# Half of the recurrent merge gate by seven products instead of eight, woven into the branch projections, with one pool for weights and activations

## The chip, the cores and the metric

The kernel runs on one core of a Trainium2 chip. Times are device microseconds of one launch. Its engines are TensorE (PE, matrix products), VectorE (DVE), ScalarE (ACT), GpSimd (POOL) and SyncE (SP, here only a queue that issues transfers). Each runs its own instructions in the order in which they were written, and waits on semaphores for the others.

## The reference

One encoder block on 256 tokens of width 2048, in fp32. `u`, `g_lru` and so on are column blocks of one input projection of width 13312.

```python
xn = rms_norm(x, norm_pre_w);  z = xn @ w_in
u_lru, g_lru, q, k, v, g_attn, m_lru, m_attn = jnp.split(z, split_at, axis=-1)
u = centred_depthwise_conv(u_lru, conv_w, conv_b)                # 4 taps
h = rg_lru(u, ..., reverse=False) + rg_lru(u, ..., reverse=True) # gates, then a scan over tokens
y_a = h * silu(g_lru)
q, k = partial_rope(q), partial_rope(k)                          # 16 heads, 4 kv heads of 128
y_b = windowed_gqa(q, k, v, sink) * silu(g_attn)                 # |i-j| <= 128
merged = sigmoid(m_lru) * (y_a @ w_proj_a) + sigmoid(m_attn) * (y_b @ w_proj_b)
out = x + rms_norm(merged @ w_out, norm_post_w)
```

## The kernel before

All products are fp32 by three: weights and activations are split into a high part (a cast to fp32r) and a low part (the rest), and a product is wh·xh + wh·xl + wl·xh.

*Steps and halves.* The weights come from DRAM in steps of 1 MB, in the order of a plan (`load_plan`). Each step has two halves of 128 x 1024. For each half ACT casts `wh` from the raw weights (line L229, issued four halves ahead) and DVE subtracts `wl` (L231, three halves ahead), and then PE multiplies. There are three kinds of step:

- `blk`: one block of 128 output columns, weights stationary. A step has 16 matmuls of 512 columns (high and low activations side by side, L261) and 16 of 256 columns (low weights, L259).
- `quad`: a quarter of the rows for 512 output columns, activations stationary, 24 matmuls of 512 columns (L234 to L236). Four quads make a chunk.
- `part`: half of one of the seven products of a `Seven`, 12 matmuls of 512 columns.

A `Seven` computes a 256 x 2048 by 2048 x 1024 product, cut into 2 x 2 blocks, by seven block products m1 to m7 instead of eight. Its activations are four blocks of x or sums of them (s1 to s4, made by `sums_of`), its weights are blocks or sums of blocks. The sums of weights are made on the way in: a cell (`x` or `y`) holds two 512 KB tiles, and transfers issued on POOL add the next block to it in place. Two Sevens exist: `am`, the second half of the attention merge gate, and `om`, the first half of w_out.

*Ticks.* Everything that isn't a step's own work is a function filed under a tick, `at(tick, fn)`, and is written out when the half of that number is written. In each half come, in this order: transfers for the step three ahead (and accumulates for the step five ahead), the functions due, the cast of the half four ahead, the subtract of the half three ahead, and the half's matmuls. That order is the order on every engine; nothing is moved later.

*Stages.* First the first four pairs' inputs `u` (quads); then for i = 0 to 7 pairs of `blk` steps for the two gates gl and ga and for u, with the recurrent pairs (`lru_pair(n, b)`: conv at b, gates' products, sigmoids, decays, `scans` at b+18, output) spread over ticks; then k, v; then q with the 16 heads, between them chunks of the recurrent gate (ml) and of w_proj_a (pa); then the attention gate (ma and the Seven `am`) with w_proj_b (pb); then w_out. A head filed at b has its scores on PE at b, exponentials on ACT at b+2, `normalise` at b+3 (DVE divides the probabilities p by their sum, L820), `flip` at b+5 (PE transposes p into pt), and `values` at b+9. A conv is four taps on DVE: L626 multiplies and adds the bias, L628 adds the other three. `x_sums(q)` makes the sums of x for the Seven: an addition of high and low part (L337), three more operations (L319 to L321) and, a tick later, the split into parts; it stores them to DRAM (`away`), and `x_sums_back` loads them when they are needed.

*Memory.* Activations live in a ring of 34 units of 4 KB a partition, raw weights in three tiles of 8 KB, `wh` and `wl` in five tiles each of 4 KB. In PSUM there are four single banks and two pairs of banks.

Of the kernel before, what the change touches and what calls it, by code (L numbers as in the profile page):

```python
# [27 lines left out]
UNITS = 34  # L29
# [4 lines left out]
LRU0 = 12  # L34
# [41 lines left out]
def load_plan():  # L76

    plan = []

    def quad(m, c):  # L80
        plan.extend(("quad", m, c, i) for i in range(4))

    def pair(m, c, n):
        plan.extend(("blk", m, c + (n + i) * P, 0) for i in range(2))

    def mixed(m, c, order):
        for o in order:
            a, i = o.split(".")
            if a in SEVEN:
                plan.append(("part", m, c, a, int(i)))  # L90
            else:
                w, w0 = CHUNKS[a[0]]
                plan.append(("quad", w, w0 + int(a[1]) * 512, int(i)))

    quad("w_in", U0)
    for i in range(8):
        if i in EARLY:
            quad("w_in", ML0 + EARLY.index(i) * 512)
        pair("w_in", GL0, 2 * i)
# [6 lines left out]
    for i in range(4):
        pair("w_in", Q0, 4 * i)
        pair("w_in", Q0, 4 * i + 2)
        quad(*MID[i])
    for m, c in MID[4:]:  # L110
        quad(m, c)
    mixed("w_in", MA0 + 1024, GATE)
    mixed("w_out", 0, OUT)
# [15 lines left out]
def body(ctx, tc, x, xT, wall, wlru, pvec, npost, ident_d, mask_d, rope_d, out):  # L129
# [3 lines left out]
    ring = ctx.enter_context(tc.tile_pool(name="ring", bufs=3))  # L133
# [55 lines left out]
    flat = lambda t: t.rearrange("p a b -> p (a b)")  # L189
# [12 lines left out]
    def cell(i):  # L202
        m, c, a, q = plan[i][1:]
        return groups[m, c].cells[SEVEN[a][1], q]

    def chained(i):
        return plan[i][0] == "part" and SEVEN[plan[i][3]][1] != "z"

    def fetch(i, lead):
        if i >= len(plan) or i in raws:  # L210
            return
        if chained(i):
            if lead == 5 and plan[i][3] in ("m6", "m7", "m4"):
                load(cell(i), plan[i], True)
        elif lead == 3:
            raws[i] = ring.tile([P, 2048], F32, tag="raw", name=f"raw{i}", bufs=3)
            nc.sync.dma_start(raws[i], wall[row[content(plan[i])]])

    def split(q, c=0, w=1024, cast=nc.scalar.copy, only=None):
# [6 lines left out]
        raw = flat(cell(i)[h]) if chained(i) else raws[i][:, h * 1024:(h + 1) * 1024]  # L226
        hs, ls, raw = wh[:, c:c + w], wl[:, c:c + w], raw[:, c:c + w]
# [5 lines left out]
    def mm3(ps, wh, wl, xh, xl, start, stop):  # L233
        nc.tensor.matmul(ps, wh, xh, start=start, stop=False)  # L234
        nc.tensor.matmul(ps, wh, xl, start=False, stop=False)  # L235
        nc.tensor.matmul(ps, wl, xh, start=False, stop=stop)  # L236
# [73 lines left out]
    def sums_of(name, src, sums, psum):  # L310
# [3 lines left out]
        f = half_unit(f"{name}f", "uu", F32).rearrange("p a (b c) -> p (a b) c", b=2)  # L314
        t = unit(name, F32R, (P, 4, 2, P))
        sums[int(name[2:])] = t

        def make(a21):
# [3 lines left out]
            soon(lambda: parts_of(t[:, :, 0], t[:, :, 1], f))  # L322

# [8 lines left out]
    away = [dram.tile([P, 4 * 2 * P], F32, name=f"away{q}") for q in range(8)]  # L332
    xsum = {}

    def x_sums(q):
        a = half_unit(f"xa{q}", "uu", F32)
        nc.vector.tensor_tensor(a, xs[q][:, :, 0].bitcast(F32), xs[q][:, :, 1].bitcast(F32), ALU.add)  # L337
        sums_of(f"xx{q}", a, xsum, False)
        soon(lambda: nc.sync.dma_start(away[q], xsum.pop(q).rearrange("p a b c -> p (a b c)").bitcast(F32)), 3)

    def x_sums_back(q):
        xsum[q] = unit(f"xb{q}", F32R, (P, 4, 2, P))
        nc.sync.dma_start(xsum[q].rearrange("p a b c -> p (a b c)").bitcast(F32), away[q])

    class Seven:
# [3 lines left out]
        def __init__(self, name, m, c, act, sums, done, double=True):  # L349
            self.name, self.act, self.sums, self.done, self.double = name, act, sums, done, double  # L350
            self.weights, self.cells, self.ps = ("part", m, c), {}, {}
            groups[m, c] = self
# [3 lines left out]

        def start(self, where, q):

            self.cells[where, q] = [unit(f"{self.name}{where}{q}{h}") for h in "ab"]
            load(self.cells[where, q], (*self.weights, "m1" if where == "x" else "m3", q))  # L360

        def second(self, q):

            load(self.cells["x", q], (*self.weights, "m5", q), True)

        def rows(self, a, i):
            if a[0] == "a":
                t, b = int(a[1]) - 1, int(a[2]) - 1
                src = self.act[i][:, b, :, t * P:(t + 1) * P]
            else:  # L370
                src = self.sums[i][:, SUMS.index(a)]
            return src[:, 0], src[:, 1]

        def half(self, m, q, h, wh, wl):
            fresh, last = q == 0 and h == 0, q == 1 and h == 1
            if fresh and self.double and m in ("m5", "m3"):

                if m == "m5":
                    self.pair = banks(f"{self.name}{m}", (P, 2, 512))
                self.ps[m] = self.pair[:, int(m == "m3")]  # L380
            elif fresh:
                self.ps[m] = bank(f"{self.name}{m}", (P, 512))
            for j in range(2):
                ah, al = self.rows(SEVEN[m][0], 4 * q + 2 * h + j)
                sl = slice(j * 512, (j + 1) * 512)
                mm3(self.ps[m], ah, al, wh[:, sl], wl[:, sl], fresh and j == 0, last and j == 1)
# [3 lines left out]
        def temp(self, name):  # L390
            return small.tile([P, 512], F32, tag="uu", name=f"{self.name}{name}", bufs=2)

        def after(self, m):
            ps, done = self.ps, self.done
            if m == "m1":
                self.m1 = small.tile([P, 512], F32, tag="upad", name=f"{self.name}c", bufs=2)
                nc.scalar.copy(self.m1, ps.pop("m1"))
            elif m == "m2":
                done(0, 0, ps.pop("m2"), self.m1, 1)
            elif m == "m6":  # L400

                self.u = small.tile([P, 512], F32, tag="upad", name=f"{self.name}u", bufs=2)
                nc.vector.tensor_tensor(self.u, ps.pop("m6"), self.m1, ALU.add)
                v = self.temp("v")
                nc.vector.tensor_tensor(v, ps["m5"], self.u, ALU.add)
                done(0, 1, ps.pop("m3"), v, -1)
# [28 lines left out]
    raws[0] = ring.tile([P, 2048], F32, tag="raw", name="raw0", bufs=3)  # L435
    for j in range(4):
        (nc.scalar if j == 1 else nc.sync).dma_start(xt[0][:, j], xT[0, :, j])
        nc.sync.dma_start(raws[0][:, j * 512:(j + 1) * 512], wall[0, :, j * 512:(j + 1) * 512])
    for i in (1, 2):
        for j in (0, 2):  # L440
            nc.sync.dma_start(xt[i][:, j:j + 2], xT[i, :, j:j + 2])
            if j == 0:
                raws[i] = ring.tile([P, 2048], F32, tag="raw", name=f"raw{i}", bufs=3)
            for c in ((j, j + 1), (j + 1, j + 2)) if i == 1 else ((j, j + 2),):
                cs = slice(c[0] * 512, c[1] * 512)
                nc.sync.dma_start(raws[i][:, cs], wall[i, :, cs])
# [111 lines left out]
    def scaled(dst, ps, then=lambda: None):  # L558
# [47 lines left out]
    def lru_pair(n, b):  # L606
# [12 lines left out]
        def conv(j):  # L619
# [6 lines left out]
            nc.vector.tensor_scalar(u, up[:, j, 0:S], cw[:, 0:1], cb, ALU.mult, ALU.add)  # L626
# [480 lines left out]
```

## Time and profile before

| | before |
|---|---|
| median of 3 runs | 900.45 us (899.63 to 901.24) |
| profiled execution | 899.96 us, span 898.2 us, clock 0.998 |
| PE busy | 888.4 us (99%), 4614 matmuls |
| DVE busy | 712.8 us (79%) |
| ACT busy | 572.4 us (64%) |
| POOL busy | 30.7 us (3%) |
| DMA | 197.38 MB, mean 220 GB/s |

The span runs from the first to the last instruction, and the profiled time is 1.8 us longer. Busy times of different engines overlap. A row of a group gives line, engine, operation, out<-in, count, then busy time and the mean of one in ns, then idle time before it. A row of a timeline or a chain gives the start and the length in us. A row of windows gives the stretch, its length, and for each engine the busy time with its instruction count.

### The profile page before, as it was taken

Reading aid. Unit: us, or ns where it says so; the run is one execution under the profiler, and the core shown is the slowest. Engines: PE = TensorE matmul, PEld = TensorE weight load, DVE = VectorE, ACT = ScalarE, POOL = GpSimd, SP = SyncE. Lnnn points to the kernel's source line nnn. Section 1 sums busy time; section 2 is a strip of 40 time slices with the busy share of each in tenths; the row PEclk is TensorE's granted clock in tenths of the full one; section 3 lists DMA queues with packets and bytes.
Section 4 is the critical chain, followed back from the end, with each engine's and each line's share of the span. In section 5 each row is a group of like instructions: output and inputs, shape, how many; then the busy total and the mean of one; then the engine's idle time right before and its main releaser. Section 6 shows DMA issues by size and latency. Waiting matters only on the chain.

```text
span 898.2 us, 12207 instructions
## 1 busy us (share of the span) xinstructions
PE 888.4 (99%) x4614; PEld 761.6 (85%) x4614; DVE 712.8 (79%) x1006; ACT 572.4 (64%) x798; POOL 30.7 (3%) x56
## 2 busy tenths in 40 slices
PE   9999999999999999999999999999999999999996
PEld 8888888888898898888888888888888888888885
DVE  6896978697979889887788979866667569778786
ACT  7688586858677977854655445554566556545764
POOL 0000000000000000000000000000002110001200
PEclk9999999999999999999999999999999999999999
DMA  9764555546465463555655455455899898797992
GB/s 338 256 237 176 190 208 191 189 158 213 158 229 185 179 211 141 188 193 205 217 183 207 169 170 205 171 204 175 280 388 261 294 292 255 260 318 264 225 312 94
DMA packets 35963, 197.38 MB, mean 220 GB/s; under 512 B 4000, under 2 KB 4768, under 8 KB 17856
## 3 DMA queue, kind: packets, MB, share of 16 engines
q1 hardware_dynamic: 30720, 179.06, 54.9%
q0 software_dynamic: 4608, 16.78, 9.9%
q10 hardware_dynamic: 576, 0.76, 0.3%
q8 instruction: 36, 0.59, 0.3%
q14 instruction: 23, 0.19, 0.1%
HBM read 190.29 MB, written 6.29 MB: 219 GB/s over the span
## 4 chain that ended last, share of the span: by engine, by line
PE 98%; DMA 1%; DVE 0%; ACT 0%; SPq 0%; DVEq 0%; issue 0%
PE q L261 7%; PE ga L261 7%; PE gl L261 7%; PE u L261 5%; PE gl L259 3%; PE ga L259 3%; PE q L259 3%; PE u L259 3%; PE u_ps L529 2%; PE k L261 2%; PE omm L235 1%; PE omm L236 1%; PE amm L235 1%; PE amm L236 1%; PE omm L234 1%; PE amm L234 1%
## 5 line engine op out<-in xcount | busy, mean ns | idle before, releaser
L229 ACT CAST wh<-raw 128x1024 fp32r<-128x1024 f32 (+1 forms) x291 | 300.0, 1041 | 178.9 <-PE q L261 25.6
L231 DVE TENSOR_TENSOR wl<-raw,wh 128x1024 fp32r<-128x1024 f32 (+1 forms) x292 | 348.1, 1204 | 67.8 <-ACT wh L229 65.3
L261 PE MATMUL q<-xs,wh 128*128 128x512 f32 x256 | 62.8, 391 | 0.0
L261 PE MATMUL ga<-xs,wh 128*128 128x512 f32 x256 | 62.4, 391 | 0.0
L261 PE MATMUL gl<-xs,wh 128*128 128x512 f32 x256 | 62.4, 391 | 0.0
L261 PEld LDWEIGHTS gl<-xs,wh 128*128 128x128 f32 x256 | 46.9, 188 | 9.0
L261 PEld LDWEIGHTS ga<-xs,wh 128*128 128x128 f32 x256 | 46.9, 188 | 8.9
L261 PEld LDWEIGHTS q<-xs,wh 128*128 128x128 f32 x256 | 46.7, 188 | 8.8
L261 PE MATMUL u<-xs,wh 128*128 128x512 f32 x192 | 46.8, 391 | 0.0
L261 PEld LDWEIGHTS u<-xs,wh 128*128 128x128 f32 x192 | 35.2, 188 | 6.7
L259 PE MATMUL q<-xs,wl 128*128 128x256 f32 x256 | 34.4, 284 | 0.0
L259 PEld LDWEIGHTS q<-xs,wl 128*128 128x128 f32 x256 | 33.1, 191 | 1.3
L259 PEld LDWEIGHTS gl<-xs,wl 128*128 128x128 f32 x256 | 33.0, 191 | 1.2
L259 PEld LDWEIGHTS ga<-xs,wl 128*128 128x128 f32 x256 | 33.0, 191 | 1.2
L259 PE MATMUL gl<-xs,wl 128*128 128x256 f32 x256 | 33.7, 283 | 0.0
L259 PE MATMUL ga<-xs,wl 128*128 128x256 f32 x256 | 33.5, 283 | 0.0
L259 PEld LDWEIGHTS u<-xs,wl 128*128 128x128 f32 x192 | 24.8, 191 | 0.9
L259 PE MATMUL u<-xs,wl 128*128 128x256 f32 x192 | 25.2, 283 | 0.0
L628 DVE SCALAR_TENSOR_TENSOR uu<-upad,pv,uu 128x256 f32<-128x256 f32 x48 | 23.3, 485 | 2.3
L651 ACT ACTIVATE gr<-gate,pv 128x256 f32<-128x256 f32 x32 | 15.3, 477 | 4.7 <-PE gate L236 4.7
L236 PE MATMUL gate<-ul,lwl 128*128 128x256 f32 x64 | 18.1, 283 | 0.0
L235 PE MATMUL gate<-ul,lwh 128*128 128x256 f32 x64 | 18.1, 283 | 0.0
(507 smaller groups left out, 2099.3 us busy)
## 6 DMA issues: line engine op xcount, KB each, us to landing
raw<-wall_dram SPq DMA_DIRECT2D x141, 1024.0 KB, 4.8
lraw<-wlru_dram SPq DMA_DIRECT2D x8, 512.0 KB, 5.7
away<-xx SPq DMA_DIRECT2D x8, 512.0 KB, 2.7
xb<-away SPq DMA_DIRECT2D x8, 512.0 KB, 7.1
raw<-wall_dram SPq DMA_DIRECT2D x8, 256.0 KB, 5.2
xr<-x_dram SPq DMA_DIRECT2D x4, 512.0 KB, 13.4
amx0a<-wall_dram POOLq DMA_DIRECT2D x3, 512.0 KB, 7.9
amx0b<-wall_dram POOLq DMA_DIRECT2D x3, 512.0 KB, 10.1
```

The source lines that it names most:

```text
L229: cast(hs, raw)
L231: nc.vector.tensor_tensor(ls, raw, hs.bitcast(F32), ALU.subtract)
L234: nc.tensor.matmul(ps, wh, xh, start=start, stop=False)
L235: nc.tensor.matmul(ps, wh, xl, start=False, stop=False)
L236: nc.tensor.matmul(ps, wl, xh, start=False, stop=stop)
L259: nc.tensor.matmul(ps[:, 1], wl[:, sl], a[:, 0], start=False, stop=False)
L261: nc.tensor.matmul(ps, wh[:, sl], a, start=k == 0, stop=k == KT - 1)
L529: nc.tensor.matmul(ups[b // 2][:, b % 2, m], w[:, sl], a[:, n], start=k == 0 and w is wh and m == 0, stop=stop)
L628: nc.vector.scalar_tensor_tensor(u, up[:, j, tap:tap + S], cw[:, tap:tap + 1], u, ALU.mult, ALU.add)
L651: nc.scalar.activation(v["gr"][:, 2 * d + j], ps[:, 0], AF.Sigmoid, bias=pv[:, PV_BR + b:PV_BR + b + 1])
```

## The change

- The second half of the recurrent merge gate (columns 1024 to 2047 of ml, two chunks of quads) becomes a third Seven, `L`. Its 14 parts stand between the `blk` steps of i = 2 to 7 (`EARLY_L`). The plan has 170 steps instead of 164: 64 quads (72 before), 64 blks, 42 parts (28 before). The names of the others are now `A` and `O`.
- A part's two halves share one tick. The recurrent pairs start at ticks 12, 28, 45, 62, 78, 93, 108 and 121 (before 12, 28, 44, 60, 76, 88, 100 and 112).
- The sums of x are made at ticks 24, 30, 36, 42, 48, 54, 60 and 65 instead of between the q steps. They are stored in another layout, and a part that needs sums loads its 512 KB (`x_sum`), four steps ahead: eight loads for `L` and eight for `A`. In these two m1's weights are the first content of cell `x`, and m5's are added to it.
- One pool of 50 units of 4 KB holds activations, raw weights, `wh` and `wl`. A raw step is two tiles and two 512 KB transfers. SP issues 357 transfers instead of 216, and POOL 48 accumulates instead of 32.
- The products m6, m7 and m4 accumulate in m1's bank and m3 in m5's, and ACT copies what is needed of a bank before the next is added. A Seven has three operations on DVE for its sums (seven before) and three copies on ACT (one before).
- The first tap of a conv goes from DVE to ACT, the other three come a tick later. The second half of the gates' products comes a tick later, and what follows it too.
- The row scaling of q falls away: its factor goes into the scale of the scores' reduction (`rtok_sc`). Normalising goes from DVE (b+3) to ACT (b+4); the flip on PE stays at b+5, values come at b+10.
- The order of the last stages is one list: q0 p0 q1 p1 q2 p2 q3 p3 and then the attention gate's chunks, parts and w_proj_b. So no chunk of ml stands among the q steps.

The core of the diff:

```diff
-UNITS = 34
+UNITS = 50
-MID = [("w_in", ML0 + 1024), ("w_proj_a", 0), ("w_proj_a", 512), ("w_in", ML0 + 1536), ("w_proj_a", 1024),
-       ("w_proj_a", 1536)]
+EARLY_L = {(2, 3): "m1.0", (2, 5): "m1.1", (3, 1): "m2.0", (3, 3): "m2.1", (3, 5): "m5.0", (4, 1): "m5.1", (4, 3): "m3.0",
...
+XSUM = (24, 30, 36, 42, 48, 54, 60, 65)
+LRU = (12, 28, 45, 62, 78, 93, 108, 121)
+SEVENS = {"L": ("w_in", ML0 + 1024), "A": ("w_in", MA0 + 1024), "O": ("w_out", 0)}
...
+        for j, c in enumerate([GL0 + 2 * i * P, GA0 + 2 * i * P] + [U0 + (2 * i + 4) * P] * (i < 6)):
+            for n in range(2):
+                plan.append(("blk", "w_in", c + n * P, 0))
+                if (i, 2 * j + n) in EARLY_L:
+                    a, q = EARLY_L[i, 2 * j + n].split(".")
+                    plan.append(("part", "L", a, int(q)))
...
-    ring = ctx.enter_context(tc.tile_pool(name="ring", bufs=3))
+    def raw_units(i):
+        raws[i] = [unit(f"raw{i}_{h}", F32, (P, 1024)) for h in range(2)]
+        return raws[i]
...
-            parts[q] = [ring.tile([P, 1024], F32R, tag=f"w{s}", name=f"w{s}{i}_{h}", bufs=5) for s in "hl"]
+            parts[q] = [unit(f"w{s}{i}_{h}", F32R, (P, 1024)) for s in "hl"]
...
+            b = {"m6": "m1", "m7": "m1", "m4": "m1", "m3": "m5"}.get(m, m)
+            fresh, last = q == 0 and h == 0 and b == m, q == 1 and h == 1
...
-            nc.vector.tensor_scalar(u, up[:, j, 0:S], cw[:, 0:1], cb, ALU.mult, ALU.add)
-            for tap in range(1, 4):
-                nc.vector.scalar_tensor_tensor(u, up[:, j, tap:tap + S], cw[:, tap:tap + 1], u, ALU.mult, ALU.add)
+            nc.scalar.activation(u, up[:, j, 0:S], AF.Identity, bias=cb, scale=cw[:, 0:1])
+            def taps():
+                for tap in range(1, 4):
+                    nc.vector.scalar_tensor_tensor(u, up[:, j, tap:tap + S], cw[:, tap:tap + 1], u, ALU.mult, ALU.add)
+            soon(taps)
...
+    for n in range(8):
+        behind(XSUM[n], lambda n=n: x_sums(n))
...
-            for t in range(2):
-                nc.vector.tensor_scalar(v["p"][:, t], v["p"][:, t], rd[:, t:t + 1], None, ALU.mult)
+            soon(lambda: [nc.scalar.activation(v["p"][:, t], v["p"][:, t], AF.Copy, scale=rd[:, t:t + 1]) for t in range(2)])
...
-            at(b + 9, values)
-            at(b + 10, gate_out)
+            at(b + 10, values)
+            at(b + 11, gate_out)
```

Where the order on an engine moves, first DVE behind the scans of the first recurrent pair (gr0, its last scan and the sum of both directions in sg0; `uu2` is the conv of the second pair, lwl2 and ul2 its gates' weights and inputs, wl16_1 the second half of step 16). Before:

```order
L673 SCALAR_TENSOR_TENSOR gr0_724<-a0_811,gi0_725 128x256
L231 TENSOR_TENSOR wl16_1_974<-raw16_888,wh16_1_973 128x1024
L162 TENSOR_TENSOR lwl2_1000<-lraw2_840,lwh2_999 128x1024
L231 TENSOR_TENSOR wl17_0_1003<-raw17_934,wh17_0_1002 128x1024
L678 TENSOR_TENSOR gr0_724<-gr0_724 128x512
L679 TENSOR_TENSOR sg0_730<-gr0_724,sg0_730 128x512
L162 TENSOR_TENSOR ul2_1022<-uu2_936,ul2_1022 128x512
L231 TENSOR_TENSOR wl17_1_1026<-raw17_934,wh17_1_1025 128x1024
```

The same place on DVE after the change (xa1 and xx1 are x_sums 1):

```order
L659 SCALAR_TENSOR_TENSOR uu2_971<-upad2_463,pv_73,uu2_971 128x256 x3
L232 TENSOR_TENSOR wl16_1_1006<-raw16_1_917,wh16_1_1005 128x1024
L340 TENSOR_TENSOR xa1_1043<-xs1_137 128x512
L321 TENSOR_TENSOR xa1_1043<-xa1_1043 128x256
L322 SCALAR_TENSOR_TENSOR xa1_1043<-xa1_1043 128x128
L323 SCALAR_TENSOR_TENSOR xa1_1043<-xa1_1043 128x128
L161 TENSOR_TENSOR lwl2_1034<-lraw2_859,lwh2_1033 128x1024
L232 TENSOR_TENSOR wl17_0_1040<-raw17_0_967,wh17_0_1039 128x1024
L709 TENSOR_TENSOR gr0_728<-gr0_728 128x512
L710 TENSOR_TENSOR sg0_734<-gr0_728,sg0_734 128x512
L161 TENSOR_TENSOR ul2_1065<-uu2_971,ul2_1065 128x512
L161 TENSOR_TENSOR xx1_1045<-xa1_1043,xx1_1045 128x4x128
```

The four operations of x_sums 1 now stand between two subtracts, its split follows, and the last three taps come behind the scans.

On DVE ahead of the scans of the third pair (gr4, gi4, th4), after the change; wl31 reads the cell tiles Lx1a and Lx1b, so step 31 is a woven part:

```order
L232 TENSOR_TENSOR wl31_0_1825<-Lx1a_1711,wh31_0_1824 128x1024
L698 SCALAR_TENSOR_TENSOR th4_1783<-gr4_1679,th4_1783 128x1024
L741 TENSOR_TENSOR sg4_1791<-sg4_1791,sig4_1850 128x512
L232 TENSOR_TENSOR wl31_1_1853<-Lx1b_1712,wh31_1_1852 128x1024
L232 TENSOR_TENSOR wl32_0_1879<-raw32_0_1814,wh32_0_1878 128x1024
L340 TENSOR_TENSOR xa6_1903<-xs6_264 128x512
L321 TENSOR_TENSOR xa6_1903<-xa6_1903 128x256
L322 SCALAR_TENSOR_TENSOR xa6_1903<-xa6_1903 128x128
L323 SCALAR_TENSOR_TENSOR xa6_1903<-xa6_1903 128x128
L232 TENSOR_TENSOR wl32_1_1900<-raw32_1_1815,wh32_1_1899 128x1024
L232 TENSOR_TENSOR wl33_0_1935<-raw33_0_1872,wh33_0_1934 128x1024
L726 TENSOR_TENSOR gi4_1680<-gi4_1680,th4_1783 128x1024
```

Before, these rows held the subtracts of two `blk` steps, the conv of the fourth pair and gi4, and neither a part's subtracts nor sums of x.

On ACT at the first head (p0, its exponentials and the normalising with rd0), after the change:

```order
L870 ACTIVATE p0_4699,dn0_4703<-p0_4699,nm0_4701 128x256 x2
L871 ACTIVATE es0_4702<-nm0_4701,pv_73 128x2
L597 COPY q1f0_4734<-q10_4631 128x512
L230 CAST wh90_0_4736<-raw90_0_4668 128x1024
L230 CAST wh90_1_4761<-raw90_1_4669 128x1024
L878 ACTIVATE p0_4699<-p0_4699,rd0_4757 128x256 x2
L230 CAST wh91_0_4797<-raw91_0_4727 128x1024
L230 CAST wh91_1_4832<-raw91_1_4728 128x1024
L160 CAST ph0_4856<-pt0_4817 128x2x256
```

Before, the same place on ACT had casts alone between exponentials and ph0, the cast that follows the flip:

```order
L811 ACTIVATE p0_4150,dn0_4154<-p0_4150,nm0_4152 128x256 x2
L812 ACTIVATE es0_4153<-nm0_4152,pv_82 128x2
L568 COPY q1f0_4185<-q10_4076 128x512
L229 CAST wh76_0_4187<-raw76_4114 128x1024
L229 CAST wh76_1_4216<-raw76_4114 128x1024
L229 CAST wh77_0_4248<-raw77_4179 128x1024
L229 CAST wh77_1_4283<-raw77_4179 128x1024
L161 CAST ph0_4305<-pt0_4268 128x2x256
```

The two scalings (L878) have come in behind the casts of the tick before, with one half's cast between them and the tick of the flip.

More of the change, by code (lines that the diff above doesn't have):

```diff
@@ L33 @@
 G = 1
-LRU0 = 12
 HEAD0 = 5
@@ L105, in load_plan @@
     quad("w_in", V0)
[L106 to L113, printed above, removed]
+    for o in MERGE + OUT:
+        a, i = o.split(".")
+        if a[0] in SEVENS:
+            plan.append(("part", a[0], a[1:], int(i)))
+        elif a[0] == "q":
+            plan.append(("blk", "w_in", Q0 + (4 * int(a[1]) + int(i)) * P, 0))
+        else:
+            w, c = CHUNKS[a[0]]
+            plan.append(("quad", w, c + int(a[1]) * 512, int(i)))
     return plan
@@ L169, in body, with ticks @@
     now = [0]
+    def ticks(i=None):
+        return sum(1 if p[0] == "part" else 2 for p in plan[:len(steps) if i is None else i])
     def at(hs, fn):
@@ L200, in body @@
     groups = {}
-    def cell(i):
-        m, c, a, q = plan[i][1:]
-        return groups[m, c].cells[SEVEN[a][1], q]
     def chained(i):
-        return plan[i][0] == "part" and SEVEN[plan[i][3]][1] != "z"
+        return plan[i][0] == "part" and groups[plan[i][1]].where(plan[i][2]) != "z"
     def fetch(i, lead):
-        if i >= len(plan) or i in raws:
+        if i >= len(plan):
             return
[L212 to L217, printed above, removed]
+        if plan[i][0] == "part":
+            groups[plan[i][1]].fetch(plan[i], lead)
+        if lead == 3 and i not in raws and not chained(i):
+            load(raw_units(i), plan[i])
     def split(q, c=0, w=1024, cast=nc.scalar.copy, only=None):
@@ L308, in body, with sums_of @@
     SUMS = ("s3", "s1", "s2", "s4")
-    def sums_of(name, src, sums, psum):
+    def sums_of(name, src, done, f=None):
         a = src.rearrange("p a b -> p (a b)")
@@ L329, in sums_of @@
             make(a21)
[L332 to L343, printed above, removed]
+    away = [dram.tile([P, 4, 4, 2 * P], F32, name=f"away{q}") for q in range(2)]
@@ L345, in body, with __init__ @@
     class Seven:
[L349 to L352, printed above, removed]
+        def __init__(self, name, act, sums, done):
+            self.name, self.act, self.sums, self.done = name, act, sums, done
+            self.cells, self.ps, self.kept, self.ready = {}, {}, {}, set()
+            groups[name] = self
@@ L357, in start @@
         def start(self, where, q):
             self.cells[where, q] = [unit(f"{self.name}{where}{q}{h}") for h in "ab"]
-            load(self.cells[where, q], (*self.weights, "m1" if where == "x" else "m3", q))
+            load(self.cells[where, q], ("part", self.name, "m1" if where == "x" else "m3", q))
         def second(self, q):
-            load(self.cells["x", q], (*self.weights, "m5", q), True)
-        def rows(self, a, i):
+            load(self.cells["x", q], ("part", self.name, "m5", q), True)
@@ L383, in half @@
+            if fresh:
+                self.ps[b] = bank(f"{self.name}{m}", (P, 512))
             for j in range(2):
-                ah, al = self.rows(SEVEN[m][0], 4 * q + 2 * h + j)
+                ah, al = self.rows(m, q, 2 * h + j)
                 sl = slice(j * 512, (j + 1) * 512)
-                mm3(self.ps[m], ah, al, wh[:, sl], wl[:, sl], fresh and j == 0, last and j == 1)
+                mm3(self.ps[b], ah, al, wh[:, sl], wl[:, sl], fresh and j == 0, last and j == 1, b != m)
             if last:
@@ L393, in after @@
         def after(self, m):
[L394 to L397, printed above, removed]
+            ps, kept, done = self.ps, self.kept, self.done
+            if m in ("m1", "m5"):
+                self.keep(m, ps[m])
             elif m == "m2":
[L399 to L406, printed above, removed]
+                done(0, 0, ps["m2"], kept["m1"], 1)
+            elif m in ("m6", "m3"):
+                if m == "m6":
+                    self.keep("u", ps["m1"])
+                self.ready.add(m)
+                if len(self.ready) == 2:
+                    soon(lambda: done(0, 1, ps["m5"], kept["u"], -1))
@@ L442, in body @@
             if j == 0:
[L443 to L446, printed above, removed]
+                raw_units(i)
+            for c in ((0, 512), (512, 1024)) if i == 1 else ((0, 1024),):
+                nc.sync.dma_start(raws[i][j // 2][:, slice(*c)], wall[i, :, j * 512 + c[0]:j * 512 + c[1]])
     nc.sync.dma_start(xt[3], xT[3])
@@ L564, in total @@
             nc.vector.tensor_tensor(dst, ps[:, :, 0], dst, ALU.add)
-            scale(dst)
+            if rows:
+                scale(dst)
+            else:
+                then()
         if len(ps.shape) == 4:
@@ L1005, in rows_in_psum, with o_sum @@
             nc.scalar.copy(to, xr[1][q // 2][:, (q % 2) * 512:(q % 2 + 1) * 512])
-    seven = Seven("om", "w_out", 0, ms, msum, lambda t, c, ps, *a: then(lambda t, f: o_done(t, c, f), t, combine(f"of{t}{c}", ps, *a)))
+    def o_sum(t, c, ps, other, sign):
+        if other is None:
+            o_done(t, c, ps)
+        else:
+            f = small.tile([P, 512], F32, tag="p", name=f"of{t}{c}", bufs=2)
+            combine(f, ps, other, sign)
+            soon(lambda: o_done(t, c, f))
+    seven = Seven("O", ms, msum, o_sum)
     for q in range(2):
-        at(b - 16 + 4 * q, lambda q=q, s=seven: s.start("x", q))
-        at(b - 12 + 4 * q, lambda q=q, s=seven: s.second(q))
-        at(b - 4 + 4 * q, lambda q=q, s=seven: s.start("y", q))
-    add_mixed(seven, OUT, lambda _, c: add_rows(f"o{c}_", ms, lambda t, ps: o_done(t, c, ps), c == 3, c == 3))
+        at(b - 16 + 4 * q, lambda q=q: seven.start("x", q))
+        at(b - 12 + 4 * q, lambda q=q: seven.second(q))
+        at(b - 4 + 4 * q, lambda q=q: seven.start("y", q))
+    add_all(OUT, lambda _, c: add_rows(f"o{c}_", ms, lambda t, ps: o_done(t, c, ps), c == 3, c == 3))
     assert [s[0] for s in steps] == [p[0] for p in plan]
-    for i, (_, half) in enumerate(steps):
+    tick = -1
+    for i, (kind, half) in enumerate(steps):
         for h in range(2):
-            now[0] = hs = 2 * i + h
+            new = h == 0 or kind != "part"
+            tick += new
+            now[0], hs = tick, 2 * i + h
             if h == 0:
-                fetch(i + 3, 3)
-                fetch(i + 5, 5)
-            if hs in first:
-                first.pop(hs)()
+                for lead in (3, 4, 5):
+                    fetch(i + lead, lead)
+            if new and tick in first:
+                first.pop(tick)()
             if hs < FIRST:
                 split(hs + 4)
-            for fn in due.pop(hs, ()):
-                fn()
+            if new:
+                for fn in due.pop(tick, ()):
+                    fn()
             if hs >= FIRST:
@@ L1031, in body @@
                     split(hs + 3, only="l")
-            if hs in last:
-                last.pop(hs)()
+            if new and tick in last:
+                last.pop(tick)()
             half(h, *parts.pop(hs))
```

224 lines of the change are left out of this document (122 added, 102 removed).

## The prediction

> **What bounds the kernel now.** I read the page first: the busy line and the chain that ended last.
>
> ```profile
> span 898.2 us, 12207 instructions
> PE 888.4 (99%) x4614; PEld 761.6 (85%) x4614; DVE 712.8 (79%) x1006; ACT 572.4 (64%) x798; POOL 30.7 (3%) x56
> PE 98%; DMA 1%; DVE 0%; ACT 0%; SPq 0%; DVEq 0%; issue 0%
> ```
>
> TensorE (PE) is busy for all but 10 us, and the chain that ends last is PE for 98%. Then the waits, asked for PE alone:
>
> ```profile
> PE spin L426 <- POOL eps L422: 1.0, 1, 1.0
> PE u_ps L529 <- DVE wh L229: 0.9, 1, 0.9
> ```
>
> These are all its waits: two, at the start. After about 10 us nothing ever keeps PE waiting. So the time falls only by what PE no longer does, and rises only where another engine becomes late for it. Both have to be priced. What a product costs is read from the chain in order of time (start, length, what), here in the stage of the attention merge gate:
>
> ```profile
> 662.97 0.23 PE amm L235
> ...
> 665.69 0.23 PE ma__6213 L235
> ...
> 671.13 0.23 PE amm L235
> ```
>
> Each row is the first second-of-three matmul of its step. From the first part (amm) to the quad (ma) lie 2.72 us for 12 matmuls of 512 columns, from there to the next part 5.44 us for 24: 0.2267 us each in both. (The group rows give 391 ns for one, because they overlap.) A quad step costs 5.44 us, a part 2.72 us.
>
> **The change, part by part.**
>
> *PE.* The second half of the recurrent merge gate was two chunks of four quads: 8 x 24 = 192 matmuls. It becomes 14 parts of 12: 168. That is 24 matmuls fewer, 24 x 0.2267 = 5.44 us. No other matmul appears or goes: projections, gates, scores, transposes and the other Sevens keep theirs. The first part of the sum is -5.44 us, and all of it lies on the path.
>
> *What must keep up.* Every 1024-column half of weights needs a cast on ACT (three to four halves ahead) and a subtract on DVE (three ahead), in whatever step. The number of halves rises from 328 to 340 while PE's time falls, so 12 more of each. These and the other operations that the change touches:
>
> ```profile
> L231 DVE TENSOR_TENSOR wl<-raw,wh 128x1024 fp32r<-128x1024 f32 x284 | 342.6, 1219 | 67.0 <-ACT wh L229 64.6
> L229 ACT CAST wh<-raw 128x1024 fp32r<-128x1024 f32 x284 | 295.6, 1051 | 177.8 <-PE q L261 25.6 <-issue 13.2 <-PE ma__5968 L236 12.2
> L820 DVE TENSOR_SCALAR p<-p,rd 128x256 f32<-128x256 f32 x32 | 9.9, 351 | 0.6
> L626 DVE TENSOR_SCALAR uu<-upad,pv 128x256 f32<-128x256 f32 x16 | 6.4, 402 | 0.0
> L560 DVE TENSOR_TENSOR q0f<-q0f,rbc 128x512 f32<-128x512 f32 x2 | 1.4, 693 | 0.1
> L651 ACT ACTIVATE gr<-gate,pv 128x256 f32<-128x256 f32 x32 | 15.3, 477 | 4.7 <-PE gate L236 4.7
> ```
>
> DVE gains 12 x 1.22 = 14.6 us of subtracts. It loses the normalising (9.9), the first conv tap (6.4) and the row scaling of q (8 x 0.69 = 5.5): 7 us less in all, and it has 21% idle. ACT gains 12 x 1.05 = 12.6 us of casts, the 32 normalisings and 16 taps at about the 0.48 us of L651 (23 us), and a few copies of sums: some 40 us on 572, with 898 there. The totals are free; the places are not.
>
> ```profile
> core 0: us, PE busy (x) PEld busy (x) DVE busy (x) ACT busy (x) POOL busy (x), PEclk, DMA share, GB/s
> 79.00:115.00 36.00, 36.00 (x216) 32.10 (x215) 31.87 (x42) 23.45 (x32) 0.14 (x2) 1.00 0.56 197
> 257.00:293.00 36.00, 36.00 (x216) 32.10 (x216) 31.25 (x41) 28.36 (x40) 0.14 (x2) 1.00 0.52 180
> 408.00:431.00 23.00, 23.00 (x103) 19.07 (x102) 16.25 (x21) 12.57 (x15) 0.00 (x0) 1.00 0.58 209
> 675.00:698.00 23.00, 23.00 (x103) 19.02 (x103) 15.69 (x16) 13.71 (x16) 4.37 (x5) 1.00 1.02 257
> ```
>
> The first two windows are the branch projections: DVE is busy 31 to 32 of 36 us there. In the query stage (third) it is 16 of 23, with ACT at 13. The change moves work *into* the first stage: the eight x_sums leave the query stage for ticks 24 to 65, and the 14 parts are woven in there, each asking for two subtracts in 2.72 us. A projection step gives 5.54 us for two (16 matmuls of 512 columns at 0.2267 and 16 of 256 in 1.91, which the chain shows below).
>
> *Sums of x.* The one x_sums that I take a price from:
>
> ```profile
> 423.77 0.69 DVE L337 TENSOR_TENSOR xa<-xs 128x512 f32<-128x512 f32 x1
> 424.49 0.42 DVE L319 TENSOR_TENSOR xx0f<-xa 128x256 f32<-128x256 f32 x1
> 424.95 0.29 DVE L320 SCALAR_TENSOR_TENSOR xx0f<-xx0f,xa 128x128 f32<-128x128 f32 x1
> 425.27 0.29 DVE L321 SCALAR_TENSOR_TENSOR xx0f<-xx0f,xa 128x128 f32<-128x128 f32 x1
> 425.48 1.22 DVE L231 TENSOR_TENSOR wl<-raw,wh 128x1024 fp32r<-128x1024 f32 x1
> 426.62 0.68 DVE L162 TENSOR_TENSOR xx<-xx0f,xx 128x512 fp32r<-128x512 f32 x1
> ```
>
> From the first start to the next subtract 1.71 us, and 0.6 more a tick later: 2.3 us, eight times, where DVE is fullest. What cover is there? The crowded place around the first pair's scans on DVE, and PE's chain where it reads two of these halves:
>
> ```profile
> 97.15 1.20 DVE L231 TENSOR_TENSOR wl<-raw,wh 128x1024 fp32r<-128x1024 f32 x1
> ...
> 102.47 1.22 DVE L231 TENSOR_TENSOR wl<-raw,wh 128x1024 fp32r<-128x1024 f32 x1
> ```
>
> ```profile
> 100.91 1.91 PE ga L259 x16
> ...
> 108.87 0.96 PE ga L259 x8
> ```
>
> The first of these subtracts (wl16_1) ends at 98.35 and is read in the second half of the first run, at 100.91 + 0.95 = 101.86: 3.5 us early, the least in this stage. The other (wl17_1) ends at 103.69 for 108.87: 5.2 us early. By the order shown for after, x_sums 0 (tick 24) now stands ahead of both, x_sums 1 (tick 30) between them, and two first taps (0.40 each) are gone. If nothing drains in between, wl16_1 keeps 3.5 - 2.3 + 0.8 = 2.0 us, wl17_1 5.2 - 4.6 + 0.8 = 1.4. So no stall, or up to 0.6 where DVE has to wait for ACT, which now makes the first tap. The second place is ticks 54 to 75: x_sums 5 to 7, the third pair's scans, the fourth's conv and the first parts of the Seven, with their two subtracts in 2.72 us. My own count of DVE's work there, by these durations, starts a subtract up to 6.9 us late, against a cover of three halves, 3 x 2.77 = 8.3, less 1.2 for the subtract itself: 7.1. So 0, or up to 1.5 if the order falls badly. Elsewhere the count stays under 5. Both places stand just at their cover, so I take about the middle of 0 to 2.1: 1.0 us.
>
> *Taps and normalising on ACT* are hidden by ACT's idle time (row L229, 178 us idle before the casts alone). If that cover fails, the flip on PE waits (rival 2). Sigmoids of the second gate a tick later, and values later, have no reader that is near. *Accumulation in a shared bank*: m6 may begin only when ACT has copied m1. The rows of OUT and the table put at least two other steps between, over 5 us, against a copy of 0.6. Nothing. *The pool of units* takes raws, casts and sums in one ring: a raw now waits for whichever unit falls free. SP runs three steps ahead (3 x 5.44 = 16 us), and loads land in 5 us. Nothing, unless a unit is held long; 0 to 1 us, in the range.
>
> *DMA.* SP issues 357 transfers instead of 216. One issue on SP, and the page's list of issues with their median time to landing:
>
> ```profile
> 201.67 0.33 SPq L217 DMA_DIRECT2D raw<-wall_dram  x1
> ```
>
> ```profile
> raw<-wall_dram SPq DMA_DIRECT2D x141, 1024.0 KB, 4.8
> omx0a<-wall_dram SPq DMA_DIRECT2D x1, 512.0 KB, 4.1
> omx0b<-wall_dram SPq DMA_DIRECT2D x1, 512.0 KB, 4.9
> omx1a<-wall_dram SPq DMA_DIRECT2D x1, 512.0 KB, 5.7
> omx1b<-wall_dram SPq DMA_DIRECT2D x1, 512.0 KB, 6.5
> omx1b<-wall_dram POOLq DMA_DIRECT2D x3, 512.0 KB, 11.8
> ```
>
> 141 more at 0.33 are 47 us, spread over 898. The four omx pieces, issued one after the other on SP, land 0.8 us apart, so a piece adds no fixed time to the one behind it, and two halves should land where one 1 MB load did, near 4.9 against 4.8. The accumulates of the new Seven go to POOL, five steps ahead (the shortest mix in that stage, three projections and two parts, 22 us), against 12 us to land. POOL's conv memsets ahead of them wait for a conv that is then ten steps old. Nothing.
>
> [...]
>
> *The sum:* profiled execution 899.96 - 5.44 + 1.0 = 895.5. The median of the runs shown is 0.5 us above the profiled one: 896.0.
>
> **The rivals.**
>
> 1. *DVE eats the gain.* Both crowded places miss by their upper ends (2.1), and parts elsewhere in ticks 54 to 122, at 2.72 us for two subtracts, miss by a few tenths each: 14 x 0.15 = 2.1. Time 900.45 - 5.44 + 4.2 = 899.2. For it: 31.87 of 36 us. Against: the conv tap leaves that stage's DVE, and each woven part stands between two projections, whose 11.1 us ask for four subtracts (4.9 us).
>
> 2. *PE waits at the flip* (slower). After the exponentials DVE had done the normalising at tick b+3, two ticks before the flip on PE. Now ACT does it at b+4, one tick before, behind the casts of the ticks before. The exponentials of a head on ACT:
>
> ```profile
> 631.43 0.51 ACT L811 ACTIVATE p<-p,nm 128x256 f32<-128x256 f32 x1
> ...
> 632.43 0.28 ACT L812 ACTIVATE es<-nm,pv 128x2 f32<-128x2 f32 x1
> 633.77 1.06 ACT L229 CAST wh<-raw 128x1024 fp32r<-128x1024 f32 x1 [1.06 <-issue]
> ```
>
> That is 1.3 us plus 1.06 idle and a cast, of some 2.75 us a tick. Two scalings of 0.48 fit, unless another head's exponentials and a q copy share the tick. It decides from a miss of 5.44 / 16 = 0.34 us at each of 16 heads. If ACT were one cast late each time, 1.05 us: 16 x 1.05 = 16.8, less 5.4: 911.8; at half of the heads 900.45 - 5.44 + 8.4 = 903.4.
>
> 3. *The halves cost a fixed time.* If two pieces did not overlap, a step's load would last 2 x 4.1 = 8.2 us (omx0a twice) against PE's 5.54: 2.7 us late at each of the 136 unchained steps, 360 us. The rows omx0b to omx1b speak against it. In the last stage, where the DMA share is 1.02, a milder form could cost 2 to 6 us: 897 to 901.
>
> 4. *No stall at all*: 900.45 - 5.44 = 895.0, inside the range of my own forecast.
>
> **How the numbers follow.** My forecast with rival 4 has 0.72 (893.9 to 897.5 as its own range: the full gain with half a microsecond of scatter either way, and the gain less 2.5). Rival 1 has 0.16 (897.5 to 900.8), rival 2 has 0.06, rival 3 has 0.06, nearly all in its mild form. The range runs to 900.9: it leaves out rival 2, a piece of 3 and what beats the full gain, about 0.12. This kernel's runs spread by 0.2%, 1.8 us, so "same" is 898.65 to 902.25. Faster: 0.72 + a third of rival 1 + a third of 3 = 0.79. Same: two thirds of rival 1 and some of 2 and 3, 0.13. Slower: 0.08.
>
> **What would show it.** Matmul rows on PE fall by 24, and the span by 3 to 5.5 us. New rows among PE's waits would name the place: gl, ga or u on DVE wl near 97 to 110 us or 150 to 210 us (my stall and rival 1); pt on ACT p between 440 and 650 us (rival 2); DVE or ACT waiting on DMA raw (rival 3). DVE in the first stage's windows should rise above 90% of PE's time, and fall under 65% in the query stage. I am wrong if PE's waits sum to more than 3 us, or if the time does not fall although there are none: then a matmul would cost more than in the rows above.

## The result: slower, by two places where PE waits and the half clock behind them

The changed kernel takes 906.05 us (905.41 to 906.78) against 900.34 us of the kernel before: ratio 1.0063, interval 1.0046 to 1.0081. Forecast were 896.0 us, between 893.9 and 900.9. First its page: span, busy line and chain.

```profile
span 904.5 us, 12540 instructions
PE 889.1 (98%) x4590; PEld 760.2 (84%) x4590; DVE 699.3 (77%) x958; ACT 597.6 (66%) x869; POOL 44.7 (5%) x72
PE 88%; DMA 6%; DVE 3%; issue 2%; ACT 1%; POOLq 0%; ACTq 0%; SPq 0%; DVEq 0%
```

PE has 24 matmuls fewer and is busy as long as before. The chain now leaves PE for 12% of the span. All waits of PE (in total, times, longest):

```profile
PE ga L261 <- DVE wl L232: 2.8, 3, 2.2
PE u_ps L555 <- DVE wh L230: 1.4, 1, 1.4
PE Om L236 <- ACT wh L230: 1.1, 1, 1.1
PE spin L451 <- POOL eps L447: 1.0, 1, 1.0
PE Om L237 <- DVE wl L232: 1.0, 2, 0.5
PE Lm L237 <- DVE wl L232: 0.5, 1, 0.5
PE u_ps L555 <- DVE xs L480: 0.2, 1, 0.2
```

They are 6 us more than before, and the missing gain is 11 (5.7 slower where 5.4 faster was the saving). The windows at the two places show the rest (stretch, length, then PE busy; the third number from the end is the granted clock):

```profile
core 0: us, PE busy (x) PEld busy (x) DVE busy (x) ACT busy (x) POOL busy (x), PEclk, DMA share, GB/s
200.00:209.00 9.00, 5.97 (x31) 4.41 (x30) 8.43 (x13) 4.00 (x6) 0.14 (x2) 1.00 0.35 140
209.00:213.00 4.00, 4.00 (x16) 3.27 (x15) 3.96 (x6) 3.97 (x6) 0.00 (x0) 0.57 0.32 106
861.00:864.40 3.40, 1.85 (x7) 0.86 (x5) 1.46 (x2) 0.99 (x2) 0.86 (x1) 1.00 1.07 280
864.40:871.40 7.00, 6.43 (x14) 4.75 (x15) 6.58 (x7) 5.74 (x9) 0.00 (x0) 0.51 1.05 273
```

At 200 us PE idles 9.00 - 5.97 = 3.0 us and then runs at 0.57 of its clock for 4 us, another 4 x 0.43 = 1.7. At 861 us it idles 1.55 + 0.57 us, and the 6.43 us in which it is busy at 0.51 of its clock cost another 6.43 x 0.49 = 3.2. That is 4.7 + 5.3 = 10.0 us. With 0.2 at 299 us (one of the ga waits) and 0.7 at the start, -5.4 + 10.0 + 0.9 = 5.5. The medians differ by 5.7, the two profiled spans by 6.3.

**The first place** is the crowded one that the prediction named, ticks 60 to 66. DVE, its row of work there, and PE's chain behind it:

```profile
203.55 1.22 DVE L232 TENSOR_TENSOR wl<-raw,wh 128x1024 fp32r<-128x1024 f32 x1
204.68 0.69 DVE L340 TENSOR_TENSOR xa<-xs 128x512 f32<-128x512 f32 x1
...
206.40 0.68 DVE L161 TENSOR_TENSOR ul<-uu,ul 128x512 fp32r<-128x512 f32 x1
207.00 1.22 DVE L232 TENSOR_TENSOR wl<-raw,wh 128x1024 fp32r<-128x1024 f32 x1
```

```profile
208.28 1.39 PE ga L261 x8
209.67 3.24 PE ga L263 x8
```

The four operations of x_sums 7 (L340 and the three after it, 204.68 to 206.48) stand ahead of the subtract that ends at 208.22, and PE starts at 208.28. Its eight matmuls of 512 columns behind that take 3.24 us instead of 8 x 0.2267 = 1.81.

**The second place** is in the output stage. ACT's casts of raw weights wait for transfers, 2.7 to 3.1 us each, and the subtracts and PE behind them:

```profile
854.95 1.05 ACT L230 CAST wh<-raw 128x1024 fp32r<-128x1024 f32 x1 [2.73 <-DMA raw<-wall_dram]
859.55 1.05 ACT L230 CAST wh<-raw 128x1024 fp32r<-128x1024 f32 x1 [3.07 <-DMA raw<-wall_dram]
863.40 1.04 ACT L230 CAST wh<-raw 128x1024 fp32r<-128x1024 f32 x1 [2.80 <-DMA raw<-wall_dram]
```

### The profile page after: what moved, and what is told of

It is laid out like the page before. It is cut to its first block, busy times and chain, and to the rows that moved or that the text cites. A ratio compares the mean times of both kernels' runs of the same rounds, so it can differ in the third digit from the quotient of the medians.

```text
span 904.5 us, 12540 instructions
## 1 busy us (share of the span) xinstructions
PE 889.1 (98%) x4590; PEld 760.2 (84%) x4590; DVE 699.3 (77%) x958; ACT 597.6 (66%) x869; POOL 44.7 (5%) x72
## 4 chain that ended last, share of the span: by engine, by line
PE 88%; DMA 6%; DVE 3%; issue 2%; ACT 1%; POOLq 0%; ACTq 0%; SPq 0%; DVEq 0%
PE q L263 6%; PE ga L263 6%; PE gl L263 6%; PE u L263 4%; DMA raw<-wall_dram 4%; PE q L261 3%; PE ga L261 3%; PE gl L261 3%; PE u L261 2%; PE k L263 2%; PE Am L236 1%; PE Am L237 1%; PE Am L238 1%; PE u_ps L555 1%; PE Lm L237 1%
## 5 line engine op out<-in xcount | busy, mean ns | idle before, releaser
L232 DVE TENSOR_TENSOR wl<-raw,wh 128x1024 fp32r<-128x1024 f32 (+1 forms) x276 | 327.7, 1203 | 67.7 <-ACT wh L230 58.0
L230 ACT CAST wh<-raw 128x1024 fp32r<-128x1024 f32 (+1 forms) x275 | 276.2, 1038 | 54.6 <-DMA raw<-wall_dram 33.5
L160 ACT CAST ph<-pt 128x512 fp32r<-128x512 f32 x16 | 9.4, 586 | 55.2 <-PE pt L884 55.2
L864 DVE CUSTOM_DVE_ANT_0 p<-sc,mask,pv 128x256 f32<-128x256 f32 x32 | 16.1, 540 | 18.7 <-PE sc L238 18.7
L160 ACT CAST ms<-mt 128x512 fp32r<-128x512 f32 x8 | 4.7, 588 | 28.5 <-PE mt L942 28.5
```

Source lines behind the costliest of these rows:

```text
L160: nc.scalar.copy(h, src)
L230: cast(hs, raw)
L232: nc.vector.tensor_tensor(ls, raw, hs.bitcast(F32), ALU.subtract)
L864: nc.vector.tensor_tensor_reduce(p[:, t], sc[:, t], mask[:, t], rtok_sc[:, t:t + 1], sk, ALU.add, ALU.max, m[:, t:t + 1])
```

## Experiments

All are against the kernel before, run beside them at 899.5 to 900.0 us.

**Sums moved, raw loads whole, both, and halves in the kernel before.**

```diff
-XSUM = (24, 30, 36, 42, 48, 54, 60, 65)        # e1, e3
+XSUM = (20, 23, 26, 40, 44, 48, 52, 56)
-UNITS = 50                                      # e2, e3
+UNITS = 44
-        raws[i] = [unit(f"raw{i}_{h}", F32, (P, 1024)) for h in range(2)]      # e2, e3
+        whole[i] = ring.tile([P, 2048], F32, tag="raw", name=f"raw{i}", bufs=3)
+        raws[i] = [whole[i][:, h * 1024:(h + 1) * 1024] for h in range(2)]
...
-            nc.sync.dma_start(raws[i], wall[...])     # e4, in the kernel before
+            for h in range(2):
+                nc.sync.dma_start(raws[i][:, hs], wall[...][:, hs])
```

> The changed kernel with the eight sums of x made at other ticks: 20, 23, 26, 40, 44, 48, 52, 56 instead of 24, 30, 36, 42, 48, 54, 60, 65. In the trace of the changed kernel PE loses 5.1 us between 200 and 213 us (three waits for a late subtract, 3.5 us, and 3.4 us at half clock behind them). Theory S (sums 6 and 7 on DVE overfill that place): these waits vanish, the stretch near 860 us stays, time 906.05 - 5.1 = 901, between 900 and 902. Rival W (the woven parts' subtracts and the taps that moved a tick later do it): the sums bring 4.6 us of DVE work there, W leaves half of the loss or more, 903.5 to 906.

> The changed kernel with raw weights in a ring of three 8 KB tiles again, one 1 MB transfer a step, and 44 units instead of 50 (the same memory). In the trace of the changed kernel PE loses 5.8 us between 861 and 872 us, where casts on ACT wait for raw weights that take up to 18 us to land beside the accumulates. Theory P (rows of 4 KB a partition get half of the share that rows of 8 KB get beside the accumulates' 4 KB): that loss vanishes, time 906.05 - 5.8 = 900, between 899.5 and 901.5; the place at 200 us stays. Rival U (raws wait for a free unit, not for bandwidth; with fewer units for the rest no better): 905 to 908. Rival O (the new order of the output stage, with two accumulated parts in a row, asks for more than the queues give in any shape): 905 to 907.

> Both edits together. Theories S and P: no wait of PE of more than 0.5 us is left, time 906.05 - 5.1 - 5.8 = 895.2, between 894.5 and 896.5, below the kernel before by 5. Rivals W and U or O: 900 to 906.

> The kernel before with each 1 MB load of raw weights issued as two of 512 KB (4 KB a partition each, into the same tile). Nothing else changes. Theory P: in the output stage of the kernel before subtracts came only 0.1 to 0.6 us early; loads at half the share make PE wait there, 3 to 8 us with the half clock behind it, time 903.5 to 908. Rivals U and O: the loads land as before within 1 us, time 900.3 plus or minus 1.

e1 took 900.91 us (ratio 1.0016, 1.0007 to 1.0025), 5.1 below the changed kernel, or 4.3 when each is taken against the kernel before beside it. S stands: the sums filled that place. Waits of 0.9 us stay there, and 1.0 near 296 us. e2 took 905.05 (1.0055, 1.0038 to 1.0071), e3 900.05 (1.0006, 0.9997 to 1.0015), e4 899.38 (0.9997, 0.9988 to 1.0006). So P fell, in both kernels: 512 KB pieces cost the kernel before nothing, and 1 MB transfers alone don't free the output stage.

**The order of the output stage, and the norm's weights earlier.** e5, e6 and e7 have e1's edit too. The first line is a part of the list `OUT`.

```diff
-Om2.0 Om2.1 Om7.0 Om7.1 o3.1                    # e5, e7 (e8: the reverse, in the kernel before)
+Om2.0 Om2.1 Om7.0 o3.1 Om7.1
-    at(b + 12, load_tail)                       # e6, e7
+    at(b + 8, load_tail)
-LRU = (12, 28, 45, 62, 78, 93, 108, 121)        # e7
+LRU = (12, 28, 45, 64, 80, 95, 110, 122)
```

> The changed kernel with the sums moved (as in e1_sums_moved, 900.91) and one swap in the order of the output stage: o3.1 stands between m7.0 and m7.1 again, as in the kernel before. In e1_sums_moved PE loses 5.6 us between 840 and 880 us beside raw loads that land late. Theory O (four parts in a row, two of them accumulated, ask for 4 MB and two accumulates within 11 us): the accumulate of m7.1 is issued 5.4 us later and a quad's time stands between, the loss falls by at least 4 us, time 895 to 897. Rivals U (a raw waits for a unit) and N (the two loads of the norm's weights, 1 MB, come in the middle of it): 900 to 901.5.

> The changed kernel with the sums moved, and the two 512 KB loads of the output norm's weights four ticks earlier (ahead of the first m5 part instead of behind o2.3). Nothing else. Theory N: they compete with the raw loads behind o2.3; earlier, the loss of 5.6 us near 850 us falls by 2 us or more, time 896 to 899. Theory O: within 1 us of e1_sums_moved, 900 to 902.

> The changed kernel with the sums moved, the swap of e5_order, the early loads of e6_norm_early, and the recurrent pairs from the fourth on one or two ticks later (12, 28, 45, 64, 80, 95, 110, 122), so that a pair's three taps no longer fall into the same ticks as the scans of the pair before. e1_sums_moved still loses 1.3 us near 200 us and 1.1 us near 300 us to late subtracts. If O holds and taps beside scans make these two: 900.91 - 5.6 - 2 = 893.3, between 892.5 and 895.5. If O falls: 899 to 901.

> The kernel before with one swap: m7.1 stands directly behind m7.0, ahead of o3.1, as in the changed kernel. Nothing else; the same work. Theory O: the same place makes PE wait here too, with the half clock behind it 2 to 6 us, time 901.5 to 905.5. Rivals U and N: 899.5 plus or minus 0.8.

e5 took 904.23 us (1.0040, 1.0025 to 1.0055), 3.3 worse than e1, and e8 899.87 (0.9997, 0.9987 to 1.0006): O fell. Why the swap is worse here stays open; the two profiled executions differ by only 1.5 us (903.96 and 902.50). The order has a second difference, o2.3 ahead of m3.0, which no run turns back alone; e10 below keeps both and loses nothing by them. e6 took 898.96 (0.9983, 0.9974 to 0.9993): N is right for 2.0 us (2.5 against the kernel before beside each). e7, with the swap in it, took 901.32 (1.0012, 1.0002 to 1.0022) where 899 to 901 was said for O falling, but its waits at 200 and 296 us are gone: the later ticks of the pairs from the fourth on remove them. That it was their taps beside the scans is argued, since the ticks move the whole pairs. In e1 and e7 the longest wait of PE (2.5 and 1.9 us) is for L758, with which DVE empties a product's bank; it stands there behind subtracts that came late behind a raw load (in e1 a cast at 854.50 us had waited 4.04 us for one).

What was left was seen on the SP queue. What SP waited for between 805 and 865 us, in the changed kernel:

```profile
SPq L205 <- PE o__7617 L238: 15.4, 2, 10.7
SPq L205 <- DVE wl L232: 15.0, 3, 6.3
SPq L205 <- PE Om L238: 10.9, 3, 4.8
SPq L983 <- DVE wl L232: 7.1, 1, 7.1
SPq L983 <- PE o__7617 L238: 6.2, 1, 6.2
...
```

and in the kernel before:

```profile
SPq L217 <- DVE wl L231: 51.9, 8, 15.3
SPq L949 <- PE omm L236: 1.2, 1, 1.2
...
```

Before, a raw load waits only for the subtract that empties its tile. With one pool it often gets a unit that last held a cast or a subtract's result, and waits until PE has read that (the rows with PE); and the norm's loads (L983) wait likewise and hold every raw load behind them on SP. What that does to landing: two loads issued between 819 and 824 us in the kernel before, and the two issued between 844 and 846 in the changed kernel (issues, KB each, median us to landing):

```profile
raw<-wall_dram SPq DMA_DIRECT2D x2, 1024.0 KB, 8.3
```

```profile
raw<-wall_dram SPq DMA_DIRECT2D x2, 512.0 KB, 16.6
```

In between POOL begins a run of twelve accumulates (825 us in both). From 833 to 846 us of the changed kernel the two queues moved (MB, then share of the engines):

```profile
q0 software_dynamic: 481, 1.75, 67.9%
q1 hardware_dynamic: 485, 1.79, 36.9%
```

Equal bytes in equal numbers of packets, 136 GB/s each: beside the accumulates SP's loads got half there, by which I estimate 3.8 us for 512 KB. For those bytes the accumulates kept the engines busy 1.8 times as long (67.9% against 36.9%). Three more runs follow from this:

```diff
-    at(b + 12, load_tail)                       # e9: e3 and this; e10: e9 and the LRU ticks of e7
+    at(b + 8, load_tail)
-UNITS = 34                                     # e11, in the kernel before
+UNITS = 40
-            raws[i] = ring.tile([P, 2048], F32, tag="raw", name=f"raw{i}", bufs=3)
+            raws[i] = [unit(f"raw{i}_{h}", F32, (P, 1024)) for h in range(2)]
```

> The changed kernel with the sums moved, raw weights in their own ring of three 1 MB tiles (44 units for the rest) and the norm's weights loaded four ticks earlier. With the ring alone (e3_both) the loads of o3.0, m2.0 and m2.1 stood on SP behind the norm's loads, which waited for a unit until 828 us; with the early norm alone (e6_norm_early) the raws themselves waited for units that PE still held. Theory Q (SP's queue stands still behind waits for units, so these three loads leave after the accumulates have begun at 821 us and then alternate with them): with both they leave before 822 and land before 833, the loss near 850 us falls under 1 us, time 895.5 to 897.5. Rival B (the output stage lacks bandwidth whenever they leave): 899 to 901.

> e9_ring_norm with the recurrent pairs at 12, 28, 45, 64, 80, 95, 110, 122. In e7_all, with these ticks, the losses at 200 and 300 us fell from 2.4 to 0.3 us. Q: 894 to 896.2, about 1.3 below e9_ring_norm. Rival B: 898 to 900.

> The kernel before with raw weights out of the ring of three: they take pairs of units from a pool of 40 instead of 34 units (the same memory), in 512 KB transfers; casts and subtracts keep their own tiles. Nothing else. On SP 56 transfers now wait for PE instead of 24. Theory Q: raw loads leave later, some of them after the accumulates of the output stage have begun, and PE waits there: 901 to 905. Rival B, or pool waits that are too short to matter: 899.3 to 900.5.

e9 took 896.26 us (0.9962, 0.9948 to 0.9977). The raw loads (L221) wait only for subtracts again (L986 loads the norm's weights, L994 rows of x):

```profile
SPq L221 <- DVE wl L235: 47.3, 7, 20.5
SPq L994 <- PE Om L241: 6.2, 1, 6.2
SPq L986 <- PE o__7367 L241: 3.9, 1, 3.9
...
```

The loss near 850 us is gone, though only two of the three loads left before 822 us. Q stands by these rows and by the time, and B is out: ring alone gave 0.9 us (e1 to e3), early norm alone 2.0 (e1 to e6), both 4.7, or 0.9, 2.5 and 4.9 against the kernel before beside each. That both give more than their sum isn't clear of the intervals, about 0.9 us either way for each run. e10 took 894.66 (0.9941, 0.9926 to 0.9956), the fastest of all. Its waits of PE are two, at the start:

```profile
PE spin L454 <- POOL eps L450: 1.0, 1, 1.0
PE u_ps L558 <- DVE xs L483: 0.2, 1, 0.2
```

899.72 - 894.66 = 5.06 us: the 5.44 of the 24 matmuls, nearly whole. e11 took 899.55 (0.9996, 0.9986 to 1.0006), and Q's 901 to 905 was wrong there: raws in the pool alone did no harm where casts and subtracts keep their own tiles; in its trace PE has two waits, 1.0 and 0.5 us, both at the start. Whether casts and subtracts in the pool would do it alone wasn't tried.

**The price of one wait.**

```diff
+    at(30, lambda: [nc.vector.tensor_scalar(mask, mask, 1.0, None, ALU.mult) for _ in range(12)])
```

> The kernel before with 12 operations added on DVE at tick 30 (the attention mask times 1.0 in place, 128 x 512, about 0.6 us each, 7.2 us in all; no value changes). They stand ahead of the subtract that came 3.5 us early, so PE should wait about 3.7 us once near 102 us. What is told apart is the price of a wait. Theory G (after a wait of that size PE is granted half its clock for 3 to 6 us, as behind the waits at 208 and 864 us of the changed kernel): the wait and 1.5 to 3 us more, time 899.7 + 5.2 to 6.7 = 905 to 906.4. Rival (a wait costs its length; the half clock there had another cause): 903.4.

It took 903.25 us (1.0035, 1.0023 to 1.0047), 3.7 more than the kernel before beside it. The twelve operations took 5.50 us, not 7.2, and PE waited once, for 2.0; the chain behind that wait:

```profile
PE ga L259 <- DVE wl L231: 2.0, 1, 2.0
```

```profile
103.69 1.22 PE ga L259 x8
104.91 5.26 PE ga L261 x16
```

and the granted clock there, 0.72 over 6 us:

```profile
103.00:109.00 6.00, 5.31 (x20) 4.40 (x21) 5.97 (x8) 0.62 (x1) 0.00 (x0) 0.72 0.52 175
```

Sixteen matmuls in 5.26 us instead of 16 x 0.2267 = 3.63: 1.6 us more, and by the clock 6 x 0.28 = 1.7. 2.0 + 1.6 = 3.6. G stands by the trace, not by its time: 905 to 906.4 was for a wait of 3.7 us, and the rival's 903.4 lies nearer only because the wait was shorter.

## Why the prediction was wrong

*Right:* a product costs 0.2267 us on the path, and the 24 that are gone are worth 5 us when nothing else comes (e10). At the first crowded place, 97 to 110 us, PE did not wait. The flips never waited for ACT: no pt stands among PE's waits, rival 2 is out. Two pieces of 512 KB cost no more than 1 MB: the kernel before runs alike with both, 899.38 us with the pieces and 899.49 without (e4, ratio 0.9997).

*Mis-sized:* the second crowded place, ticks 54 to 75. The step "0, or up to 1.5 if the order falls badly" came from a count of 6.9 us against a cover of 7.1. It was 3.0 us of idle PE. The count added up durations as if DVE were never idle. In the trace it is busy for 48.85 of the 58.2 us from 150 to 208.2 us, and waits mostly for ACT (8.5 us in all); the longest gap:

```profile
173.08 1.23 DVE L232 TENSOR_TENSOR wl<-raw,wh 128x1024 fp32r<-128x1024 f32 x1 [3.60 <-ACT wh L230]
```

That such gaps are all that the count lacked isn't shown. Where a count comes within 3% of the cover, its own error is the term.

*Missing:* the price of a wait. The sum took each late subtract at its length. Behind waits of 1.9 to 2.8 us in five traces PE ran at about half its clock for 3.4 us or longer (granted 0.57 over 4 us from 209 us in the changed kernel), and in e12 a wait of 2.0 us cost 3.6. This term alone was 1.7 + 3.2 us of the 11.

*Wrong step:* "The pool of units ... SP runs three steps ahead (3 x 5.44 = 16 us), and loads land in 5 us. Nothing, unless a unit is held long; 0 to 1 us, in the range." None of it entered the sum. Units were held long, by casts that PE had yet to read, and 5 us is a landing time of loads that meet no accumulates: 4.8 us for 1 MB, the median from 100 to 600 us of the kernel before, against 12.7 for 512 KB, that of the ten raw loads from 825 to 868 us of the changed kernel. It cost 5.3 us in the trace, and 4.7 us between e1 and e9. I had the row for it, 11.8 us of an accumulate beside loads, and used it for the accumulates alone. Rival 3 in its mild form put a loss of 2 to 6 us into this stage, but for another reason, pieces, which e4 rules out; its time, 897 to 901, was 5 us short. A loss of its size and one of rival 1's came together, which no case of mine held.

DVE rose as forecast at 79 to 115 us (32.48 of 36.00 us, 90%). The query stage begins 44 us later than before, so its old window now lies at 452 to 475 us, where DVE is busy for 13.08 of 23.00 us, 57%, as forecast; over the 192 us with the heads' flips it fell from 153.27 to 137.13 us, 71%, not under 65%. The lower end of the range, 893.9, doesn't follow from its own words (895.0 less half a microsecond is 894.5); nothing hangs on it.

## What to carry to other kernels

When buffers of different engines are put into one pool, ask for each transfer whose last read it will now wait for, and what stands behind it on its queue: a load that left before a burst of accumulates may leave inside it (here 512 KB then took 16.6 us to land, where 1 MB had taken 8.3). Work that is put where an engine is nearly full must be counted with its idle gaps, and a late operand on a PE that is never idle is to be priced with the half clock that may follow (e12: 1.6 us behind a wait of 2.0). A saving on the path is kept only if its side effects are moved out of the way: with SP freed and two lists of ticks shifted the same change gains what its arithmetic says (e10).

## What the hardware showed that I had not expected

In e12 one wait of 2.0 us was followed by half the clock for about 3.4 us, estimated from the granted 0.72 over 6 us (6 x 0.28 / 0.5); sixteen matmuls took 5.26 us instead of 3.63. In the slow stretch at 866 us of the changed kernel a matmul starts every 0.427 us, against 0.2267. Waits of 1.9 to 2.8 us were followed by such stretches in e12 and four other traces, of 3.4 or 6.8 us by such estimates (mean clock 0.995 in e12, 0.993 in the changed kernel, 0.997 in e1, 0.990 in e2, 0.996 in e7, against 0.998 in the kernel before). So were three short waits in a row: 0.5, 1.1 and 0.5 us from 861 us in the changed kernel (0.51 over 7 us) and 0.6, 1.1 and 0.7 in e5 (mean clock 0.994), about 6.8 us each. But the length doesn't decide. In e6 three waits of 0.7, 1.1 and 0.8 us, at the same place, were followed by a full clock, and one of e12's seven runs (901.69 us, mean clock 0.998 as in the kernel before) was only 2.1 us longer than that kernel, hardly more than the wait. The longest wait of all, 3.1 us in e3 near 845 us, was followed by a full clock too (two windows of e3, then two of e6):

```profile
840.00:852.00 12.00, 8.93 (x40) 7.08 (x39) 9.32 (x9) 6.90 (x9) 2.51 (x3) 1.00 1.05 315
852.00:858.00 6.00, 6.00 (x28) 4.99 (x27) 2.96 (x3) 3.01 (x5) 0.99 (x2) 1.00 1.04 295
...
856.00:861.00 5.00, 2.65 (x10) 1.31 (x8) 3.00 (x3) 2.31 (x5) 0.86 (x1) 1.00 1.06 274
861.00:868.00 7.00, 6.89 (x29) 5.47 (x30) 6.66 (x8) 5.79 (x9) 0.00 (x0) 1.00 1.03 314
```

The slow stretches lasted 3.4 us or twice that. What decides which waits are followed by one, no run here shows.
